# A hybrid attention encoder on one core: fuller contractions, split sums of squares, and other orders at the start, the openings and the end

## The chip, the core and the metric

The kernel runs on one core of a Trainium2 chip. The metric is the device time of the program in microseconds, median of several runs. The core's engines are TensorE (PE; its weight loads are shown apart as PEld), VectorE (DVE), ScalarE (ACT), GpSimd (POOL) and SyncE (SP), which here only issues transfers.

## The reference, cut to what matters

Two layers work on 528 tokens (512 and 16 learned meta tokens) of 1024 channels, in float32:

```python
h = concatenate([meta, x], axis=1)
for l in range(DEPTH):                    # DEPTH = 2
    h = h + 0.5 * swiglu(rmsnorm(h, ...), gate, up, down)     # D_FF = 2816
    h = h + mixer(rmsnorm(h, ...), ...)
    h = h + 0.5 * swiglu(rmsnorm(h, ...), gate, up, down)
return rmsnorm(h, final_norm)[:, N_META:]

def mixer(z, ...):
    h = z @ w_in      # q,k,v,r of branch A, two low-rank decays (16 each), q,k,v of branch B, two gates
    a = gla_branch(...)        # 4 heads, chunked linear attention forwards and backwards
    b = attention_branch(...)  # 8 query heads on 2 key heads, softmax over all 528 tokens
    y = sigmoid(g_a + b0) * (a @ w_pa) + sigmoid(g_b + b1) * (b @ w_pb)
    return y @ w_out
```

In branch A the decay is log_sigmoid(lr @ w2 + b2) / 16 for either direction, and each head's output is normalised by its mean square over 128 channels. In branch B queries and keys are normalised over 64 channels.

## The kernel before, in words

Activations lie with channels on the 128 partitions and tokens along the free axis: eight chunks h(c) of 528 columns, two halves of 264. In the last layer's end only 512 tokens are kept (halves of 256).

**Precision.** A float32 product is made of three matmuls of a reduced type: each operand is split in hi (a cast on ScalarE) and lo (value minus hi, a subtraction on VectorE), and hi·hi, hi·lo and lo·hi are added in PSUM. Some small products are left in full float32: the sums of squares over channels (`means`, L388, and L1016 at the end), the decay product (L612), and the products inside branch A (L655, L691, L718, L727, L728).

**Weights.** The class `Weights` streams slabs of 128x1024 in the order of a plan. Slabs are fetched up to six and made (split) up to four ahead of their use, with four buffers each for hi and lo: the hi cast is L222, the lo subtraction L227. With the flag `by_dma` (the gate projections behind the attention) lo is made by a negation on ScalarE (L224) and an adding transfer issued by POOL (L178).

**Feed-forward.** Gate and up projections work on pairs of 128-wide column blocks with seven products of block sums in place of eight (products "1" to "7", 24 matmuls each, L502). The sums of weights come by chained adding transfers on POOL's queue (`sums`: s3 = block 21 minus block 11, s2 = block 22 plus s3, and so on; products 7, 6, 5, 3 read them), those of activations from `Norm.pair`, which prepares seven operands for each pair of chunks. Products are evaluated in an order that starts "1 2 6 5" for a group's first pair. Products 1, 6, 7 and 4 add up in one PSUM tile (snapshots by ScalarE between them, L508), 2 in a second, 5 and 3 in a third. The down projection follows in groups of 4, 4 and 3 pairs (L382); its results are scaled (L469), added to h (L478), squared (L416) and the squares added up (L420) for the next norm; `Norm.pair` casts (L433) and subtracts (L434) the next operands. `norm.rs()` makes the factors from `means`; it is asked for at high priority behind product 5 of the first pair.

**Mixer.** Projections go through `project` (L382). `gla_pair` is called for two pairs of heads: for each direction a decay product (L612), exponentials and scans (L622), decayed keys (L651) and their transposes (L655), states, then blocks from the last to the first. `attention` normalises and rotates queries and keys, and for each of 16 units of two query blocks makes probabilities (`probs`, L836 and L837) and weighted values (`weighted`): transposes (L861), split, matmuls over four blocks of 128 tokens (L878, L879), and a tail over the 16 meta tokens.

**Order.** Instructions are put in order for each engine ahead of time, by a list scheduler with priorities from the program's order and modelled durations. On the chip each engine then works strictly in that order and waits where data is late. Gate projections are taken in between the attention's units where TensorE has room.

**End.** The last down product (m = 7) is done by halves, and the final norm's factors, multiplications (L1023) and stores (L1025) follow for each half.

## Time and profile before

| | |
|---|---|
| median of three runs | 2294.09 us (2293.67 to 2300.5) |
| span of the profiled execution | 2289.1 us; its own time is not shown apart, the median is 5.0 longer |
| TensorE busy | 2225.1 us, 16548 matmuls |
| VectorE busy | 1491.3 us |
| ScalarE busy | 1214.4 us |
| POOL busy | 195.1 us |
| mean granted clock of TensorE | 0.991 |
| HBM | 264.38 MB read, 2.10 MB written |

A row of a group or of the timeline reads: start and length in us (timeline), engine, line, operation, tile written <- tiles read, shape, count. A TensorE row's length is the latency of overlapping matmuls; the distance of starts is the pitch. In brackets stands the idle time ahead of the instruction and what ended it. Lines are those of the kernel printed above.

### The profile page before, as it was taken

Reading aid. Unit: us, or ns where it says so; the run is one execution under the profiler, and the core shown is the slowest. Engines: PE = TensorE matmul, PEld = TensorE weight load, DVE = VectorE, ACT = ScalarE, POOL = GpSimd, SP = SyncE. Lnnn points to the kernel's source line nnn. Section 1 sums busy time; section 2 is a strip of 40 time slices with the busy share of each in tenths; the row PEclk is TensorE's granted clock in tenths of the full one; section 3 lists DMA queues with packets and bytes.
Section 4 is the critical chain, followed back from the end, with each engine's and each line's share of the span. In section 5 each row is a group of like instructions: output and inputs, shape, how many; then the busy total and the mean of one; then the engine's idle time right before and its main releaser. Section 6 shows DMA issues by size and latency. Waiting matters only on the chain.

```text
span 2289.1 us, 39919 instructions
## 1 busy us (share of the span) xinstructions
PE 2225.1 (97%) x16548; PEld 2108.4 (92%) x16548; DVE 1491.3 (65%) x2355; ACT 1214.4 (53%) x1785; POOL 195.1 (9%) x218
## 2 busy tenths in 40 slices
PE   5999999999999999999989999999999999999997
PEld 5999999989999999999989999998788888989896
DVE  6656567476775676565676565674768667756566
ACT  7536355344786564453565353553448946636452
POOL 1111010010000010101011110100000001101010
PEclk9999999999999999999989999999999999999999
DMA  8858562211325485766667585632113356859661
GB/s 225 236 150 224 142 175 93 74 57 56 84 56 157 117 214 153 189 180 173 181 141 202 151 219 146 170 98 74 56 65 93 74 156 152 223 149 223 159 176 61
DMA packets 91869, 327.79 MB, mean 143 GB/s; under 512 B 10214, under 2 KB 12646, under 8 KB 91688
## 3 DMA queue, kind: packets, MB, share of 16 engines
q1 hardware_dynamic: 61136, 218.26, 28.7%
q0 software_dynamic: 28800, 104.87, 25.6%
q8 instruction: 130, 2.13, 0.4%
q10 hardware_dynamic: 1752, 2.11, 0.3%
q14 instruction: 51, 0.42, 0.1%
HBM read 264.38 MB, written 2.10 MB: 116 GB/s over the span
## 4 chain that ended last, share of the span: by engine, by line
PE 89%; DVE 5%; DMA 2%; ACT 2%; issue 1%; SPq 0%; DVEq 0%; POOL 0%; ACTq 0%
PE ss L502 36%; PE ss L382 27%; PE mm L382 14%; PE sm L382 3%; PE sm L861 1%; PE sm L878 1%; DVE wlo L227 1%; PE sm L879 1%; PE ss L836 1%; DMA w<-win 1%; PE ss L837 1%; PE ss L388 1%; DMA s<-win 1%; PE ss L718 1%; DMA w<-s 1%
## 5 line engine op out<-in xcount | busy, mean ns | idle before, releaser
L502 PE MATMUL ss<-xc,whi 128*128 128x264 f32 (+1 forms) x4928 | 902.3, 285 | 26.5 <-ACT snap L508 9.7
L502 PEld LDWEIGHTS ss<-xc,whi 128*128 128x128 f32 x4928 | 766.8, 189 | 29.3 <-ACT snap L508 10.3
L502 PE MATMUL ss<-xc,wlo 128*128 128x264 f32 (+1 forms) x2464 | 702.1, 285 | 4.3 <-DVE wlo L227 4.3
L382 PE MATMUL ss<-g,whi 128*128 128x264 f32 (+2 forms) x2668 | 494.2, 301 | 0.0
L502 PEld LDWEIGHTS ss<-xc,wlo 128*128 128x128 f32 x2464 | 466.0, 189 | 5.3 <-DVE wlo L227 5.1
L382 PEld LDWEIGHTS ss<-g,whi 128*128 128x128 f32 x2668 | 388.6, 188 | 17.4
L382 PE MATMUL mm<-x,whi 128*128 128x264 f32 (+1 forms) x1712 | 383.5, 315 | 0.0
L222 ACT CAST whi<-w 128x1024 fp32r<-128x1024 f32 (+1 forms) x221 | 230.8, 1047 | 263.1 <-PE ss L382 118.7
L222 ACT CAST whi<-raw 128x1024 fp32r<-128x1024 f32 x190 | 199.3, 1049 | 299.5 <-PE mm L382 106.9
L227 DVE TENSOR_TENSOR wlo<-w,whi 128x1024 fp32r<-128x1024 f32 (+1 forms) x221 | 267.9, 1218 | 110.7 <-ACT whi L222 108.4
L382 PE MATMUL ss<-g,wlo 128*128 128x264 f32 (+2 forms) x1334 | 309.9, 301 | 0.0
L382 PEld LDWEIGHTS mm<-x,whi 128*128 128x128 f32 x1712 | 279.5, 189 | 18.8 <-issue 2.1
L382 PE MATMUL mm<-x,wlo 128*128 128x264 f32 (+1 forms) x856 | 267.2, 317 | 0.0
L227 DVE TENSOR_TENSOR wlo<-raw,whi 128x1024 fp32r<-128x1024 f32 x166 | 203.1, 1224 | 95.2 <-ACT whi L222 94.2
L382 PEld LDWEIGHTS ss<-g,wlo 128*128 128x128 f32 x1334 | 213.4, 188 | 8.7
L227 DVE TENSOR_TENSOR wlo<-s,whi 128x1024 fp32r<-128x1024 f32 x88 | 107.6, 1223 | 102.0 <-ACT whi L222 101.9
L222 ACT CAST whi<-s 128x1024 fp32r<-128x1024 f32 x88 | 92.4, 1050 | 153.6 <-PE ss L502 135.4
L382 PEld LDWEIGHTS mm<-x,wlo 128*128 128x128 f32 x856 | 160.4, 189 | 10.8 <-issue 2.2
L469 DVE SCALAR_TENSOR_TENSOR t<-ss,rs 128x528 f32<-128x528 f32 (+1 forms) x95 | 66.0, 700 | 127.8 <-PE ss L382 127.7
L173 ACT ACTIVATE s<-w 128x1024 f32<-128x1024 f32 x88 | 93.3, 1060 | 79.2 <-DMA w<-win 41.5
L178 POOL DMA_DIRECT2D s<-win x44 | 40.8, 927 | 497.0 <-ACT s L173 489.2
L508 ACT COPY snap<-ss 128x528 f32<-128x528 f32 (+1 forms) x132 | 77.2, 585 | 0.0
(235 smaller groups left out, 2660.3 us busy)
## 6 DMA issues: line engine op xcount, KB each, us to landing
w<-win SPq DMA_DIRECT2D x219, 512.0 KB, 4.7
raw<-wts SPq DMA_DIRECT2D x190, 512.0 KB, 3.4
s<-win POOLq DMA_DIRECT2D x44, 512.0 KB, 6.8
w<-s POOLq DMA_DIRECT2D x44, 512.0 KB, 5.5
w<-win POOLq DMA_DIRECT2D x44, 512.0 KB, 7.1
s<-w POOLq DMA_DIRECT2D x44, 512.0 KB, 7.4
wlo<-raw POOLq DMA_DIRECT2D x24, 512.0 KB, 4.4
h<-xt SPq DMA_DIRECT2D x3, 528.0 KB, 7.1
```

Of the source, the lines that this page charges most:

```text
L173: self.nc.scalar.activation(t, w, AF.Copy, scale=-1.0)
L178: self.nc.gpsimd.dma_start(t, src, accum_op=ALU.add)
L222: nc.scalar.copy(hi[:, cs], w[:, cs])
L227: nc.vector.tensor_tensor(lo[:, cs], w[:, cs], hi[:, cs].bitcast(F32), ALU.subtract)
L382: TE.matmul(acc.half[i][:width], lhs, rhs[:, acc.spans[i]], start=first, stop=last)
L388: TE.matmul(a, weights, x[:, hs], start=True, stop=True)
L469: V.scalar_tensor_tensor(cut(dst[rows]), pv[rows], -0.5 * f, cut(rs[rows]), ALU.mult, ALU.mult)
L502: TE.matmul(acc[:, j], a[:, j, k], b[:, at], start=bool(begin and k == 0 and i == 0), stop=k == len(x) - 1 and i == 2, skip_group_check=no ...
L508: S.copy(st[name], acc)
L718: TE.matmul(ats[:n, hh, d * n : (d + 1) * n], prods[d][1][rows, bs], prods[d][0][rows, bs], start=True, stop=True)
L836: TE.matmul(s[:n, i, :HF], lhs, kh[:, hs], start=True, stop=False)
L837: TE.matmul(s[:n, i, :HF], lhs, kl[:, hs], start=False, stop=True)
```

## The change

- `weighted`: the tail's two matmuls over 16 rows become one over 128: hi of the probabilities in rows 0 to 15, lo in rows 32 to 47, zeros elsewhere; the values stand in both places. Two halves of one buffer are used in turn.
- Decay product: weights and operand are laid out over 128 rows (hi and lo of each, the bias), in the reduced type, one matmul for each half. The low-rank projection computes hi and lo columns side by side (64 columns, two matmuls a chunk and half and no third).
- States: matmuls take all 128 rows, with zeros where a direction has no state. The four score products of a block alternate between heads.
- Sums of squares: `means` becomes `totals`: the squares are split in hi and lo, two matmuls of the reduced type each against ones; the division goes into the later steps.
- `by_dma` goes: all lo slabs are made by VectorE.
- First feed-forward: the first pair is computed from whole blocks (`Norm.whole`, `first_pair`: 192 matmuls, no sums of weights or activations); the seven operands are made behind that.
- The three other feed-forwards open with products 1 and 2 of pair 0 (the last chunk's matmuls of both at the end), then 1 and 2 of pair 1, then 6, 5, 7, 4, 3 of pair 0. For the last chunk the operands are made ahead of the square. The norm's factors are asked for behind product 6.
- End: the last three down products (m = 5, 6, 7) are done by halves, all three for the first half and then for the second; their squares are summed by TensorE in full float32, finished chunks are scaled by ScalarE, and a half is multiplied and stored in two pieces.

```diff
+        if g:
+            steps += [("P", pair, c) for c in "1265"]
+        elif begin:
+            steps += [("F", pair, "1"), ("F", pair, "2")] + [("P", pair + 1, c) for c in "1265"]
+        else:
+            steps += [("O", pair, "12")] + [("P", pair + 1, c) for c in "12"] + [("P", pair, c) for c in "65"]
...
-                if self.by_dma:
-                    nc.scalar.activation(lo[:, cs], hi[:, cs].bitcast(F32), AF.Copy, scale=-1.0)
-                    self.add(lo[:, cs].bitcast(F32), w[:, cs])
-                else:
-                    nc.vector.tensor_tensor(lo[:, cs], w[:, cs], hi[:, cs].bitcast(F32), ALU.subtract)
+                nc.vector.tensor_tensor(lo[:, cs], w[:, cs], hi[:, cs].bitcast(F32), ALU.subtract)
...
+    def totals(weights, x, kind="ss"):
+        n = x.shape[-1]
+        hi, lo = slot("t", F32R, n), slot("t", F32R, n)
+        S.copy(hi, x)
+        V.tensor_tensor(lo, x, hi.bitcast(F32), ALU.subtract)
+        acc = Acc(kind, n)
+        for b, first in ((hi, True), (lo, False)):
+            for a, hs in zip(acc.half, acc.spans):
+                TE.matmul(a, weights, b[:, hs], start=first, stop=not first)
...
         def chunk_of_pair(self, c):
-            self.square(c)
+            if c % 2 and c < KC - 1:
+                self.square(c)
             if c % 2:
                 self.pair(c // 2)
+            if c == KC - 1 or c % 2 == 0:
+                self.square(c)
...
+        def first_pair(p, m):
+            accs = [pair(m == "2") for _ in range(2)]
+            blocks = [W.op((l, f), p, m + c) for c in "12"]
+            for k, (first, second) in enumerate(zip(x, norm.second)):
+                for j, acc in enumerate(accs):
+                    for r, (hi, lo) in enumerate(blocks):
+                        for i, (a, b) in enumerate(((hi, 0), (hi, 1), (lo, 0))):
+                            for t, v in enumerate((first, second)):
+                                TE.matmul(acc[:, t, :w], a[:, j, k], v[b][:, r], ...)
+        def two_products(p, names):
...
+            for ks in (range(last), [last]):
+                for acc, at, hi, lo in work:
+                    for k in ks:
...
-                TE.matmul(z[:, i, :HF], w2t[:33, c0 : c0 + P], lr[:33, hs], start=True, stop=True)
+                TE.matmul(z[:, i, :HF], w2t[:, c0 : c0 + P], lr[:, hs], start=True, stop=True)
...
-                TE.matmul(os_, state(b)[rows, hh], qin[hh][rows, bs], start=False, stop=True)
+                TE.matmul(os_, state(b)[:, hh], qin[hh][:, bs], start=False, stop=True)
...
-                parts.append((vs[g][1], hi[:, :w], lo[:, :w]))
+                S.copy(tail[:META], tp[:META, :w])
+                V.tensor_tensor(tail[32 : 32 + META], tp[:META, :w], tail[:META].bitcast(F32), ALU.subtract)
...
+                TE.matmul(o[:, :w], vs[g][1], tail, start=False, stop=True)
...
-        W.by_dma = True
         gates += [project(x, None, "g", n=n_out) for _ in range(2 * KC - EARLY)]
-        W.by_dma = False
...
+        for i, hs in enumerate(spans):                 # closing: halves
+            for m, acc, wm in zip(late, accs, w):      # m = 5, 6, 7
...
+                    act(sq, h(m, hs), AF.Square)
+                    S.activation(h(m, hs), h(m, hs), AF.Identity, scale=gfin[:, m : m + 1])
...
+        store(0, spans[0])
+        total(1, KC - 1)
+        finish(1)
+        store(1, spans[1])
```

More of the change, by code (lines that the diff above doesn't have):

```diff
@@ L230, in make @@
             self.made += 1
-            if not isinstance(load, int) and load[2] in "12":
+            if not isinstance(load, int) and load[2] in ("1", "2"):
                 self.sums(*load, w)
@@ L503, in product_of_pair, with finished @@
                                   stop=k == len(x) - 1 and i == 2, skip_group_check=not begin)
+            finished(p, product)
+        def finished(p, product):
+            st = made[p]
+            acc = st[{"2": "Y", "5": "Z", "3": "Z"}.get(product, "X")][:, :, :w]
             def snapshot(name):
@@ L547, in down @@
             kind = "s2" if other == (m // 2 % 2 == 1) else "ss"
-            ending = g == len(GROUPS) - 1 and m == KC - 1 and done is None
+            if done is None and g == len(GROUPS) - 1 and m >= LATE:
+                if m == LATE:
+                    closing([hid[base + k] for k in range(2 * GROUPS[g])], rs)
+                return
             if first == 0:
-                sums[m] = Acc(kind, cut=ending)
+                sums[m] = Acc(kind)
             width = 2 * GROUPS[g]
-            product("ffn_w_down", sums[m], [hid[base + k] for k in range(first, last)], last - first, by_half=ending,
+            product("ffn_w_down", sums[m], [hid[base + k] for k in range(first, last)], last - first,
                     begin=first == 0, end=last == width)
-            if last < width or ending:
+            if last < width:
                 return
@@ L983, in build @@
     nc.sync.dma_start(h(1), xt[:, 1])
-    first.pair(0)
-    W.fetch(1)
+    first.whole(0)
+    W.make(2)
     for c in (2, 4, 6):
         nc.sync.dma_start(hall[:, c : c + 2], xt[:, c : c + 2])
-        first.pair(c // 2)
-    W.fetch(2)
-    nc.sync.dma_start(ct[:, C_O1024 : C_O1024 + P], const[:, C_O1024 : C_O1024 + P])
+        first.whole(c // 2)
+    W.make(4)
     for c in range(KC):
         first.square(c)
+    for j in range(KC // 2):
+        first.pair(j)
     norms = [first] + [Norm(G_NORM + i * KC) for i in range(1, 3 * DEPTH)]
```

285 lines of the change are left out of this document (200 added, 85 removed).

## The prediction

> **What bounds the kernel now.** I read the page's head, its engine table and its chain of work first, then the waits of TensorE, then the chain in order of time, and last the timeline around each place that the diff touches.
>
> ```profile
> span 2289.1 us, 39919 instructions
> PE 2225.1 (97%) x16548; PEld 2108.4 (92%) x16548; DVE 1491.3 (65%) x2355; ACT 1214.4 (53%) x1785; POOL 195.1 (9%) x218
> PE 89%; DVE 5%; DMA 2%; ACT 2%; issue 1%; SPq 0%; DVEq 0%; POOL 0%; ACTq 0%
> ```
>
> ```profile
> PE ss L655 <- DVE p L651: 11.8, 8, 2.0
> PE ss L502 <- ACT snap L508: 9.7, 1, 9.7
> PE ss L502 <- ACT whi L222: 9.2, 2, 7.8
> PE ss L502 <- ACT xc L433: 7.3, 1, 7.3
> PE ss L388 <- DVE t L420: 5.4, 3, 2.7
> ...
> PE ss L1016 <- DVE t L1013: 4.3, 2, 2.3
> ```
>
> ```profile
> 160.01 73.19 PE ss L502 x600
> ```
>
> TensorE is busy 97% of the span and is 89% of the chain: the kernel is bound by the number and pitch of its matmuls. The waits (us in total, times, longest) are only some 50 us; the largest lie at the start. The chain row gives the pitch of a full 264-column matmul in a dense stretch: 73.19 / 600 = 0.122 us. So two things can move the time: TensorE work taken away, and the stalls at start, stage openings and end.
>
> **Short contractions (the attention's tail).** Now each block of weighted values ends with two matmuls over 16 rows:
>
> ```profile
> 651.29 0.28 PE L879 MATMUL sm<-q,k 128*128 128x256 f32 x1
> 651.50 0.38 PE L878 MATMUL sm<-lr,vm 16*128 16x256 f32 x1
> 651.73 0.27 PE L879 MATMUL sm<-lr,vm 16*128 16x256 f32 x1
> 651.93 0.51 PE L382 MATMUL mm<-x,whi 128*128 128x264 f32 x2
> 652.28 0.28 PE L836 MATMUL ss<-k,p 128*128 128x264 f32 x1
> ```
>
> From 651.29 to 652.28 are 0.99 us for three full matmuls (0.36) and the two short ones: 0.63 for the pair, because the matmul before the short ones, each of them, and the first behind them all start their successor about 0.1 late. The new form is one full matmul, 0.12. Saved 0.51 here; where transposes follow, rather less, so I take 0.45 for each of 32 calls (two more calls are small): **15 us**, at most 16.3.
>
> The Trainium skill speaks against this: "TensorE: Matmul & The Clock Gate", section "Why this matters for your kernels", says that a single matmul over 32 rows takes the time of one over 128, the gain being only in running several at once. By it one matmul fewer for each of 34 calls would be all, 4 us. No start in the rows above agrees with it; I go by the rows.
>
> **The decay product (L612), sums of squares (L388), states (L728), low rank.**
>
> ```profile
> 481.94 1.05 PE L388 MATMUL ss<-t,const 128*128 128x264 f32 x4
> 482.63 0.48 PE L382 MATMUL mm<-x,wlo 128*128 128x264 f32 x1
> 482.95 0.41 PE L382 MATMUL mm<-x,whi 128*128 128x264 f32 x2
> ...
> 487.39 0.41 PE L382 MATMUL mm<-x,whi 128*128 128x264 f32 x2
> 487.73 1.16 PE L612 MATMUL ss<-lr,w 33*128 33x264 f32 x4
> 488.82 0.39 PE L382 MATMUL mm<-x,wlo 128*128 128x264 f32 x1
> 489.05 0.41 PE L382 MATMUL mm<-x,whi 128*128 128x264 f32 x2
> ...
> 522.17 0.49 PE L728 MATMUL sm<-p,q 64*128 64x128 f32 x2
> 523.00 0.48 PE L728 MATMUL sm<-p,q 64*128 64x128 f32 x2
> ```
>
> ```profile
> L382 PE MATMUL sm<-x,whi 128*32 128x264 f32 x64 | 10.3, 283 | 0.0
> L382 PE MATMUL sm<-x,wlo 128*32 128x264 f32 x32 | 6.4, 282 | 0.0
> ```
>
> L612: 1.66 us from 487.39 to 489.05 less three ordinary pitches is 1.29; the split form is two ordinary matmuls, 0.24. Saved 1.05 x 8 (two pairs, two directions, two layers) = **8.4**. L388: 481.94 to 482.95 is 1.01, less one ordinary pitch 0.89; the hi and lo form is four ordinary ones, 0.49. Saved 0.40 x 16 calls (six norms, eight heads, two key norms) = **6.4**. L728: a short pair and the full pair behind it take 0.83 (522.17 to 523.00); four full matmuls at no more than 0.122 each take 0.49. Saved 0.34 x 8 = **2.7**. Low rank: 96 matmuls become 64, 32 x 0.122 = **3.9**. The swapped order of the score products keeps their number; I give it nothing (0 to 2). Sum of TensorE work taken away: 15 + 8.4 + 6.4 + 2.7 + 3.9 = **36.4 us**.
>
> **What of that comes back as waits.** In the gated branch TensorE already waits 8 times for L651, 11.8 us: the chain of scans and exponentials is what is late there. L612, L728 and half of L388 lie in that branch, 14.3 us; what lies ahead of the chain's first matmul moves the chain too, what lies behind it only lengthens a wait. The nearest row allows anything from 0 to 14.3 lost; I take 3, since most of L612 stands ahead of its chain. The splits add a copy on ScalarE and a subtraction on VectorE to each sum of squares; in the heads other projections cover them, and without that cover they would lengthen the same waits.
>
> The larger risk is the edit that drops by_dma:
>
> ```profile
> 545.00:697.00 152.00, 151.31 (x1168) 141.84 (x1165) 112.22 (x284) 116.70 (x241) 7.42 (x9) 0.99 0.28 74
> 595.00:620.00 25.00, 24.88 (x193) 23.32 (x193) 21.23 (x57) 20.72 (x44) 1.76 (x2) 1.00 0.35 86
> ...
> L224 ACT ACTIVATE wlo<-whi x24: 1040/1062/1092, 584.1 to 1839.6; 128x1024 fp32r<-128x1024 f32 x24
> ...
> L227 DVE TENSOR_TENSOR wlo<-raw,whi 128x1024 fp32r<-128x1024 f32 x166 | 203.1, 1224 | 95.2 <-ACT whi L222 94.2
> ```
>
> 24 slabs get their low half from VectorE (1.224 each) and no longer from ScalarE (1.062) and POOL's queue. The columns after the length are TensorE, weight load, VectorE, ScalarE. In the first attention VectorE has 112.2 of 152 us; nine of the layer's twelve slabs fall there, so 123 of some 144: 85%. In the densest 25 us it has 21.2 now and gets one or two more slabs: 22.4 to 23.7 of the 23.5 that TensorE would then need. So VectorE comes level with TensorE for part of the stage, where TensorE so far waits for nothing. Bounds: 0 (ScalarE's 12.7 us of relief shortens the softmax chain) to all of the attention's gain, 16. I charge 6. Net work: 36.4 - 3 - 6 = **27.4**.
>
> **The start.**
>
> ```profile
> 0.00:40.00 40.00, 16.64 (x81) 14.58 (x82) 29.21 (x54) 31.40 (x53) 4.90 (x10) 0.87 0.84 240
> ...
> 23.00 0.28 PE L502 MATMUL ss<-xc,wlo 128*128 128x264 f32 x1
> 32.99 0.81 PE L502 MATMUL ss<-xc,whi 128*128 128x264 f32 x2 [9.71 <-ACT snap L508]
> 33.60 1.96 PE L388 MATMUL ss<-t,const 128*128 128x264 f32 x4
> ```
>
> In the first 40 us TensorE does 77 matmuls and one sum: 9.4 + 0.9 us of warm work, so 29.7 us are lost. The 9.7 are not snap's: product 6 waits for weights summed by two chained transfers. The first pair from whole blocks needs 192 matmuls for 168 (+24 x 0.122 = 2.9) but no summed weights, so the transfers of pair 1 run under them. It needs two blocks before the first k is complete: start at some 8.5 instead of 7.75. Then 192 x 0.122 = 23.4, about 2.4 more for some 24 of them at half clock (the four records of 33.60 take 1.96, those of 481.94 take 1.05), 1.5 of gaps while chunks arrive: end at 35.8. VectorE's 29.2 and ScalarE's 31.4 busy us in those 40 grow by the second halves' casts and the first pair's low parts, so pair 1's operands come late at its product 6: 3 us charged (0 to 9.7, the wait that stands there now). Lost then 35.8 + 3 - 168 x 0.122 = 18.3; gain 29.7 - 18.3 = **11** (5 to 17).
>
> **Openings with four products.**
>
> ```profile
> 1169.32 0.70 DVE L469 SCALAR_TENSOR_TENSOR t<-ss,rs 128x528 f32<-128x528 f32 x1
> 1170.17 0.78 PE L502 MATMUL ss<-xc,whi 128*128 128x264 f32 x2 [7.34 <-ACT xc L433]
> 1175.60 2.12 PE L388 MATMUL ss<-t,const 128*128 128x264 f32 x4 [2.67 <-DVE t L420]
> ```
>
> Between the layers TensorE stands 7.3 us. The profile names the cast, but the first matmul reads only the oldest operand; the eviction L469 at 1169.32 ends at 1170.02, and it frees the bank that pair 0's first product takes. That eviction is not moved, so these 7.3 us stay. Behind it 36 matmuls instead of 18 stand ahead of the last chunk, and that chunk's operand comes ahead of its square: 18 x 0.122 = 2.2 saved, part of the 2.67 too. In the two other openings the waits are the rest of L388's 5.4, 2.7 for both: I count half. Against it, the sum now needs a cast and a subtraction more, and product 7 is followed at once by 4, which must wait for the snapshot of the same bank; pair 1's product 6 can fill that (without this cover 1 us for each of three openings). 2.2 + 1.4 less 0.6: **3** (-3 to 8).
>
> **The end.**
>
> ```profile
> 2272.21 0.28 PE L382 MATMUL ss<-g,wlo 128*128 128x256 f32 x1
> 2274.43 0.70 PE L1016 MATMUL ss<-t,const 128*128 128x256 f32 x2 [1.95 <-DVE t L1013]
> 2277.45 1.02 PE L1016 MATMUL ss<-t,const 128*128 128x256 f32 x2 [2.31 <-DVE t L1013]
> ```
>
> The second half's sum now stands 3.0 behind the first; with the first half done under the second half's products it takes its place, and no squares are added between: 3.4 sooner. Two multiplications of 1024 columns (1.22 each, as L227) replace eight, about 1 sooner at the end. Against it six single sums over full-precision squares (0.45 each, half of L388's 0.89), five of them ahead of the last product, and two splits' four matmuls: 2.7; and the last transfer is twice as large. **1.5** (-1 to 4). The scaling of finished chunks moves to ScalarE, idle there; without that room 0.6 for a chunk.
>
> Costed at nothing: assembling the low-rank and decay operands, the zero fills and gfin; the projections of the same stage cover them, else some 3 us for a layer.
>
> **Sum.** 27.4 + 11 + 3 + 1.5 = 42.9. The span is 2289.1; the median of the runs shown, 2294.1, is 5.0 longer, which I take as what lies around the span. 2294.1 - 42.9 = **2251 us**. All good ends (36.4 + 17 + 8 + 4) give 2229, all bad ones (36.4 - 14.3 - 16 = 6, then + 5 - 3 - 1) 2287.
>
> **Rivals.** *VectorE takes over the attention.* Place: both attention stages; decided where it passes TensorE over the whole stage. For it: 21.2 of 25 us already. Against: no wait of TensorE for it there today, and its mean stays at 85%. The attention's 16 us go: 2251 + 10 = 2261. *The start gains nothing*: both vector engines saturate (31.4 of 40 on ScalarE) and pair 1's product 6 waits the same 9.7: 2262. *Short contractions cost nothing extra*: then the tails save 4 and not 15, L728 nothing, L612 only the repeated passes (four records at L388's 0.89 / 4 become 0.24 in all, 5.2 and not 8.4): 2251 + 17 = 2268. This is the rule of the Trainium skill's TensorE page quoted above; against it stand the starts of the tail rows. *Slower*: the sums and casts on an in-order VectorE make TensorE wait in every one of the attention's 34 weighted calls. Priced at the longest wait for L651, 2.0 us: 68, so 2251 - 6 (charged already) being replaced by it, 2313. It decides the sign from 1.5 us for each call on. Against it: 85% mean load, and a ScalarE that is relieved.
>
> **Chances.** My forecast 0.52; VectorE 0.20; start 0.12; no switching cost 0.04; slower 0.08; several losses at once, ending within 0.3%, 0.04. A difference of 0.3% (7 us) is about what a measurement can tell from none. The first four are faster: 0.88; slower 0.08. The range takes the first four cases in with their bounds: 2234 to 2272.
>
> **What would show it.** No 16-row or 33-row matmul in the list; a pitch of 0.12 around the tail; no single idle of TensorE over 5 us in the first 40 us; the 7.3 us before product 1 of layer 1 still there; VectorE at 85 to 90% in the attention. Waits of TensorE for VectorE in the attention adding up to over 16 us, or a wait of over 10 us behind the first pair, would make the number wrong.

## The result, and the profile after

The changed kernel takes 2263.92 us (median of four runs, 2259.63 to 2265.68), the kernel before 2295.72 beside it: a ratio of 0.986, 95% interval 0.984 to 0.9875. That is 1.4% faster, on the side forecast and within the range of 2234 to 2272, but 12.9 us above the 2251 predicted.

The head and the engine table of the changed kernel's page, and its waits of TensorE (us in total, times, longest):

```profile
span 2261.6 us, 39885 instructions
PE 2204.5 (97%) x16538; PEld 2102.9 (93%) x16538; DVE 1527.2 (68%) x2397; ACT 1218.3 (54%) x1824; POOL 164.7 (7%) x184
```

```profile
PE ss L764 <- DVE p L760: 12.5, 8, 2.1
PE ss L597 <- ACT whi L238: 9.5, 4, 4.7
PE ss L556 <- ACT whi L238: 8.0, 2, 7.2
PE ss L597 <- ACT snap L608: 7.4, 4, 3.8
PE ss L597 <- DVE wlo L239: 5.1, 6, 2.2
PE ss L1136 <- ACT square L387: 1.4, 1, 1.4
```

The gated branch's wait stands as before (11.8, now 12.5 at L764). The 9.7 at the start and the 7.3 between the layers are gone, and so are the waits for the squares. In their place come waits of products (L597) for weights (whi, wlo) and for snapshots (snap): 22 us, of which 18 lie behind the first group, where no such wait stood before. L597 is the old L502, L404 the old L382.

The span, 27.5 us shorter, cut at the first and last matmul of each stage (worked out from the starts in the timeline; a mixer is counted from its first projection to the start of `w_out`, which is in "all else"):

| stage | before | after | gain | predicted |
|---|---|---|---|---|
| start to the end of the first group | 160.0 | 151.3 | 8.7 | 11 |
| mixer, layer 0 | 375.2 | 366.0 | 9.2 | |
| mixer, layer 1 | 353.7 | 336.5 | 17.2 | 27.4 for both |
| first groups of the three later feed-forwards | 400.2 | 409.5 | -9.3 | +3 |
| last groups and end (from 2179.5 before) | 109.6 | 107.3 | 2.3 | 1.5 |
| all else | 890.4 | 891.0 | -0.6 | 0 |

The openings are the row with the wrong sign: 12.3 of the 15.4 us by which the span (2289.1 - 42.9 = 2246.2 predicted, 2261.6 measured) came out longer. The start adds 2.3, the mixers 1.0 and all else 0.6, and the end takes 0.8 off. That the medians differ by only 12.9 is luck: the 5.0 us taken as lying around the span came from a median and a profile of different executions. Seven later runs of the kernel before have 1.8 to 2.0 us around their spans, the changed kernel's profiled run 1.9 (2263.49 against 2261.6); with 2.0 the forecast would have been 2248.

**The start.** One row of a windows view, to be held against the row for the same 40 us before (TensorE 16.64 us, 81 matmuls), and the first long wait of the changed kernel in the timeline:

```profile
0.00:40.00 40.00, 31.39 (x228) 30.78 (x228) 31.14 (x61) 33.80 (x60) 3.69 (x8) 1.00 0.78 240
```

```profile
7.20 0.59 PE L556 MATMUL ss<-xc,whi 128*128 128x264 f32 x1 [7.20 <-ACT whi L238]
9.64 0.59 PE L556 MATMUL ss<-xc,whi 128*128 128x264 f32 x1 [0.75 <-ACT whi L238]
...
61.86 0.51 PE L597 MATMUL ss<-xc,whi 128*128 128x264 f32 x2 [3.80 <-ACT snap L608]
```

From the first matmul on, the first 40 us are nearly full, as forecast; the first pair ends at 34.8 us. A wait of 3.8 us, about the size of the 3 charged, stands at 58 us. It isn't the one that was charged: the product at 61.86 is the eighth behind the first pair, product 4 of pair 1, and it waits for a snapshot that ScalarE takes late.

**The opening between the layers**, rows of all engines from the changed kernel's timeline:

```profile
1148.40 1.06 ACT L238 CAST whi<-w 128x1024 fp32r<-128x1024 f32 x1 [1.94 <-PE ss L404]
...
1164.28 1.04 ACT L238 CAST whi<-w 128x1024 fp32r<-128x1024 f32 x1
...
1165.35 1.23 DVE L239 TENSOR_TENSOR wlo<-w,whi 128x1024 fp32r<-128x1024 f32 x1 [0.23 <-ACT whi L238]
...
1166.61 5.94 SPq L184 DMA_DIRECT2D w<-win  x4
...
1170.56 0.86 POOL L194 DMA_DIRECT2D w<-s  x1 [32.28 <-DVE c L615]
1173.27 0.89 POOL L194 DMA_DIRECT2D w<-win  x1 [1.85 <-DMA w<-win]
...
1177.05 1.04 ACT L238 CAST whi<-w 128x1024 fp32r<-128x1024 f32 x1 [2.42 <-DMA w<-s]
...
1178.14 0.51 PE L597 MATMUL ss<-xc,whi 128*128 128x264 f32 x2 [2.23 <-ACT whi L238]
...
1182.26 1.04 ACT L238 CAST whi<-w 128x1024 fp32r<-128x1024 f32 x1 [4.16 <-DMA w<-win]
...
1183.35 0.81 PE L597 MATMUL ss<-xc,whi 128*128 128x264 f32 x2 [4.70 <-ACT whi L238]
```

Read from the bottom: the product at 1183.35 waits 4.70 us for a cast of weights, and the cast at 1182.26 waits 4.16 us for the adding transfer that POOL issued at 1173.27. The product at 1178.14 depends in the same way on the transfer of 1170.56, ahead of which POOL issued nothing for 32.28 us.

POOL's row names c (L615), but the transfer doesn't read c: that is only VectorE's last instruction before it. The transfer adds to a block that SyncE has to fetch first. SyncE requests it at 1166.61, right behind VectorE's subtraction of 1165.35 (1165.35 + 1.23 = 1166.58); the waits of SyncE's queue show 18.6 us behind such a subtraction. That subtraction splits the summed weights of pair 0's product 6, and so frees one of the two buffers for short sums.

It comes that late because the slab is the fifth of the opening. Products 1 and 2 of pair 0 and 1 and 2 of pair 1 hold all four buffers of hi and lo from the cast of 1148.40 on. None of the four ends before the last chunk's matmuls, at about 1162 to 1164, and the next slab's cast starts at 1164.28.

**The tail of the attention**, now one full matmul, goes through at the ordinary pitch (0.12 to it and 0.12 from it, where the pair of 16-row matmuls took 0.63):

```profile
643.27 0.28 PE L993 MATMUL sm<-q,k 128*128 128x256 f32 x1
643.39 0.28 PE L994 MATMUL sm<-lr,vm 128*128 128x256 f32 x1
643.51 0.27 PE L976 MATMUL sm<-const,t 128*128 128x128 f32 x1
```

### The profile page after: what moved, and what is told of

It is laid out like the page before. It is cut to its first block, busy times and chain, and to the rows that moved or that the text cites. A ratio compares the mean times of both kernels' runs of the same rounds, so it can differ in the third digit from the quotient of the medians.

```text
span 2261.6 us, 39885 instructions
## 1 busy us (share of the span) xinstructions
PE 2204.5 (97%) x16538; PEld 2102.9 (93%) x16538; DVE 1527.2 (68%) x2397; ACT 1218.3 (54%) x1824; POOL 164.7 (7%) x184
## 5 line engine op out<-in xcount | busy, mean ns | idle before, releaser
L597 PE MATMUL ss<-xc,whi 128*128 128x264 f32 (+1 forms) x4720 | 865.1, 285 | 16.9 <-ACT whi L238 9.5
L597 PEld LDWEIGHTS ss<-xc,whi 128*128 128x128 f32 x4720 | 734.7, 189 | 19.7 <-ACT whi L238 10.3
L597 PE MATMUL ss<-xc,wlo 128*128 128x264 f32 (+1 forms) x2360 | 671.4, 285 | 5.1 <-DVE wlo L239 5.1
L404 PE MATMUL ss<-g,whi 128*128 128x264 f32 (+1 forms) x2620 | 482.8, 300 | 0.0
L597 PEld LDWEIGHTS ss<-xc,wlo 128*128 128x128 f32 x2360 | 446.8, 189 | 6.4 <-DVE wlo L239 6.3
L404 PEld LDWEIGHTS ss<-g,whi 128*128 128x128 f32 x2620 | 380.6, 188 | 15.7
L404 PE MATMUL mm<-x,whi 128*128 128x264 f32 (+1 forms) x1712 | 385.8, 315 | 0.0
L239 DVE TENSOR_TENSOR wlo<-raw,whi 128x1024 fp32r<-128x1024 f32 x190 | 232.1, 1222 | 105.8 <-ACT whi L238 104.8
L404 PE MATMUL ss<-g,wlo 128*128 128x264 f32 (+1 forms) x1310 | 302.2, 300 | 0.0
L404 PEld LDWEIGHTS mm<-x,whi 128*128 128x128 f32 x1712 | 281.2, 190 | 15.3 <-DVE x L393 0.2
L404 PE MATMUL mm<-x,wlo 128*128 128x264 f32 (+1 forms) x856 | 265.2, 314 | 0.0
L404 PEld LDWEIGHTS ss<-g,wlo 128*128 128x128 f32 x1310 | 209.2, 188 | 8.3
L404 PEld LDWEIGHTS mm<-x,wlo 128*128 128x128 f32 x856 | 161.2, 190 | 7.6
L527 DVE SCALAR_TENSOR_TENSOR t<-ss,rs 128x528 f32<-128x528 f32 (+1 forms) x93 | 64.6, 700 | 126.4 <-PE ss L404 126.3
L194 POOL DMA_DIRECT2D w<-win x43 | 37.8, 880 | 599.3 <-DVE wlo L239 222.3
L393 DVE TENSOR_TENSOR g<-c,g 128x528 fp32r<-128x528 f32 (+1 forms) x88 | 61.5, 699 | 22.6 <-ACT g L392 22.6
```

What stands on the lines that cost most here:

```text
L194: self.nc.gpsimd.dma_start(t, src, accum_op=ALU.add)
L239: nc.vector.tensor_tensor(lo[:, cs], w[:, cs], hi[:, cs].bitcast(F32), ALU.subtract)
L393: V.tensor_tensor(lo, src, hi.bitcast(F32), ALU.subtract)
L404: TE.matmul(acc.half[i][:width], lhs, rhs[:, acc.spans[i]], start=first, stop=last)
L527: V.scalar_tensor_tensor(cut(dst[rows]), pv[rows], -0.5 * f, cut(rs[rows]), ALU.mult, ALU.mult)
L597: TE.matmul(acc[:, j], a[:, j, k], b[:, at], start=bool(begin and k == 0 and i == 0), stop=k == len(x) - 1 and i == 2, skip_group_check=no ...
```

## The experiments

All stand against the changed kernel (2263.92 us, span 2261.6) and are edits of it. The kernel before took 2292.9 to 2293.7 us beside them and 2295.7 beside the changed kernel, so medians that differ by less than some 3 us tell nothing. Where stage lengths are compared they are cut as in the table above. "Opening sum" is the first groups of the three later feed-forwards together: 400.2 before, 409.5 after.

### The scaling of the ones moved out of the start

```diff
     def load_constants():
-        S.activation(ones64, b64, AF.Copy, scale=float(HD))
...
+        if l == 0:                       # in the attention
+            S.activation(ones64, b64, AF.Copy, scale=float(HD))
```

> The changed kernel with one instruction moved: the scaling of the 64-channel ones, which load_constants puts on ScalarE right behind the request for the constants, is made ahead of the first attention. Theory A (ScalarE stands 4.7 us for the constants' transfer at 54 to 59 us, the snapshot behind it is late, TensorE waits 3.8 us and then runs 3.4 us at half clock): the wait of 3.8 us behind the first pair goes and the time falls by 4 to 6 us. Theory B (TensorE waits there for the weights summed by chained transfers, the constants only happen to land then): a wait of about the same size stays at product 6 or 5 of pair 1, and the time moves by less than 2 us.

2262.43 us, span 2258.8. The wait of 3.80 us at product 4 of pair 1 is gone: the scaling, queued on ScalarE behind the constants' load, did hold the snapshot. But two products later, at product 6 of pair 2, 2.05 us behind a cast of summed weights stand at 62.8 us, and the first group takes 143.7 us (144.1). The transfers held the start nearly as long as the scaling did, and the time is as long as before, as the second theory had it.

### The openings with two products again

```diff
-        if g:
+        if g or not begin:
             steps += [("P", pair, c) for c in "1265"]
...
-        else:
-            steps += [("O", pair, "12")] + [("P", pair + 1, c) for c in "12"] + [("P", pair, c) for c in "65"]
```

> The changed kernel with the three later feed-forwards opened as before (products 1, 2, 6, 5 of pair 0); all else stays, the operands ahead of the last square and the split sums too. Theory A (four products ahead move product 6 of pair 0 nearer to product 6 of pair 1, and with two buffers for short sums the chained transfers of pair 1 come late): the first groups of these feed-forwards, which take 134.1, 145.5 and 129.9 us from the end of the product before, go back to 131, 141 and 126, and the time falls by 8 to 12 us. Theory B (the later square and the longer chain of the split sum hold TensorE up): the groups stay within 2 us of 134.1, 145.5 and 129.9.

Span 2249.9, opening sum 398.3 (131.0 + 141.3 + 126.0). The waits of this kernel:

```profile
PE ss L593 <- ACT xc L484: 7.3, 1, 7.3
PE ss L411 <- ACT t L406: 4.4, 3, 1.8
PE ss L593 <- ACT snap L604: 1.8, 2, 1.5
```

The waits for weights in the openings have gone and the old 7.3 us between the layers are back: the four products cost 11.2 us of opening, more than the 7.3 and the waits for squares that they remove. The median, 2260.93 (2252.08 to 2261.45), fell by only 3, not by the 8 to 12 expected: the profiled run is the fastest of the four, the others were granted a clock of 0.988 to 0.989 and not 0.992.

### The low halves by ScalarE and POOL again in the gates

```diff
+                if self.by_dma:
+                    nc.scalar.activation(lo[:, cs], hi[:, cs].bitcast(F32), AF.Copy, scale=-1.0)
+                    self.add(lo[:, cs].bitcast(F32), w[:, cs])
+                else:
                     nc.vector.tensor_tensor(lo[:, cs], w[:, cs], hi[:, cs].bitcast(F32), ALU.subtract)
```

> The changed kernel with the low halves of the late gate slabs made again by ScalarE and an adding transfer, as before. Theory A of the prediction (VectorE comes level with TensorE in the attention and costs some 6 us of its gain): 3 to 6 us faster. Theory B (VectorE has room, ScalarE was the fuller engine): within 2 us, or slower by up to 4 us since ScalarE gets 12.7 us more in each layer.

2266.41 us, span 2268.4: not faster, so the first theory fails. Attention to the last weighted values takes 232.9 us for both layers against 235.0, the projections behind it 119.9 against 116.8. The 2.1 us are no cost of VectorE: the attentions of the changed kernel hold 708 matmuls of projections, those of this kernel 687, and 21 matmuls are 2.6 us at 0.122. Together the two parts take 352.8 us here and 351.8 in the changed kernel. The densest 26 us of the changed kernel in the windows view (TensorE, weight load, VectorE, ScalarE), and of this one:

```profile
584.00:610.00 26.00, 25.88 (x210) 25.09 (x210) 25.41 (x62) 18.48 (x40) 0.00 (x0) 1.00 0.19 62
```

```profile
584.00:610.00 26.00, 25.64 (x200) 24.71 (x199) 23.11 (x61) 21.48 (x44) 1.75 (x2) 0.96 0.34 87
```

VectorE is busy 98% there after the change, and TensorE is busy 25.88 of the 26 us all the same. Here a full VectorE costs TensorE nothing that the rows show.

### Two 16-row matmuls in the tail again

```diff
...
+                parts.append((vs[g][1], hi[:, :w], lo[:, :w]))     # 16 rows each
...
-                TE.matmul(o[:, :w], vs[g][1], tail, start=False, stop=True)
```

> The changed kernel with the attention's tail as before: two matmuls over 16 rows for each of 34 calls, in one buffer. Theory A (a short contraction costs by the switch into it and out of it): 16-row matmuls with starts 0.2 us apart are back, 0.35 to 0.45 us for each of 32 calls, 11 to 15 us slower. Theory B (a short contraction costs what a full one does, only their number counts): 34 matmuls more at 0.12, 4 us slower.

2276.29 us (2267.5 to 2287.45), 12.4 slower than with one full matmul. That the 12.4 lie in the forecast's 11 to 15 says little: the runs spread by 20 us, with granted clocks from 0.984 to 0.994, and the profiled run has 26 us more at half clock than the changed kernel's, none of it in the attention. The stage itself, measured with the next experiment, is 8.4 us longer, between the two theories. The tail in the timeline:

```profile
640.82 0.28 PE L989 MATMUL sm<-q,k 128*128 128x256 f32 x1
641.03 0.38 PE L988 MATMUL sm<-lr,vm 16*128 16x256 f32 x1
641.25 0.28 PE L989 MATMUL sm<-lr,vm 16*128 16x256 f32 x1
641.45 0.33 PE L971 MATMUL sm<-const,t 128*128 128x128 f32 x1
```

640.82 to 641.45 is 0.63 for three matmuls, where three full ones take 0.36. The first short one starts 0.21 behind a full one, the second 0.22 behind the first, and the full one 0.20 behind that: each of the three starts is 0.1 late.

### The full tail issued twice

```diff
-                TE.matmul(o[:, :w], vs[g][1], tail, start=False, stop=True)
+                for i in range(2):
+                    TE.matmul(o[:, :w], vs[g][1], tail, start=False, stop=i == 1)
```

> Each tail's one full matmul over 128 rows is issued twice (its terms are then added twice). Theory A (a 16-row matmul costs by the switch between row counts, not by being one matmul more): the second full matmul costs one pitch, 34 x 0.12 = 4 us, so 4 above the after kernel's span at the same clock and 8 to 10 below the kernel with two 16-row matmuls. Theory B (a matmul over few rows takes the time of one over 128, and the cost lay in having two dependent on late operands): as long as the kernel with 16-row matmuls, the two attention stages (first probabilities to last weighted values, 123.9 and 111.1 us with one full matmul) both 6 or more longer; by A they are 2 longer each.

2269.16 us, span 2270.9, with 17 us more at half clock than the changed kernel's profile has, so the stage is compared here too, not the span. The tail in the timeline:

```profile
648.68 0.28 PE L993 MATMUL sm<-q,k 128*128 128x256 f32 x1
648.79 0.40 PE L995 MATMUL sm<-lr,vm 128*128 128x256 f32 x2
649.03 0.29 PE L951 MATMUL ss<-k,p 128*128 128x264 f32 x1
```

Two full matmuls take 0.24 (648.79 to 649.03), where the two short ones take 0.42 and delay their entry by 0.1. From the first probabilities to the last projection, both layers: 351.8 us with one full matmul, 355.5 with two, 360.2 with two of 16 rows. One full matmul more costs 3.7 (34 x 0.122 is 4.1), making the two short costs another 4.7. So it isn't the number: in this attention two 16-row matmuls between full ones cost more than two of 128 rows. By the pitches of the tail and of the score products ahead of it the difference of the last two is 8.5; the stages show 4.7. With the short ones, the other matmuls of the stage take 2.8 us less by their pitches and TensorE idles 0.9 less; why they do, no run shows.

### Pair 1's products 1 and 2 back between pair 0's steps

```diff
-            steps += [("O", pair, "12")] + [("P", pair + 1, c) for c in "12"] + [("P", pair, c) for c in "65"]
+            steps += [("O", pair, "12")] + [("P", pair, c) for c in "65"]     # 1 and 2 of pair 1 by 7 and 4, as before
```

> The three later blocks still open with products 1 and 2 of pair 0 interleaved, but pair 1's 1 and 2 move back to where pair 0's steps 7 and 4 stand, so that seven products instead of five lie between product 6 of pair 0 and product 6 of pair 1. Theory A (the openings lose by the distance: pair 1's summed weights come too late): the waits behind the opening go, the first groups of those three blocks fall from 134.1 + 145.5 + 129.9 = 409.5 us to some 398 (they were 398.3 without the four products), the span from 2261.6 to about 2250. Theory B (they lose by the interleaving itself, for instance by both banks being taken at once, wherever pair 1's products stand): they stay at 407 to 410, the span within 3 us of 2261.6.

2254.1 us, span 2252.8, opening sum 400.5 (131.8 + 142.7 + 126.0). Interleaving the two products of pair 0 is thus not what costs, as the first theory had it. With seven products between the sixes (counted from the start of pair 0's product 6 to the start of pair 1's) the openings are as long as before the change, and the 7.3 us between the layers are back.

### Three products ahead

```diff
-            steps += [("O", pair, "12")] + [("P", pair + 1, c) for c in "12"] + [("P", pair, c) for c in "65"]
+            steps += [("O", pair, "12")] + [("P", pair + 1, "1")] + [("P", pair, c) for c in "65"]     # 2 of pair 1 by 4
```

> Three products ahead of pair 0's 6 and 5: 1 and 2 of pair 0 interleaved, then 1 of pair 1; its 2 moves back to the place between 7 and 4. Six products lie between the two 6s. Theory A (distance): between the two others, first groups 399 to 404 us in all, span 2251 to 2256; the third product ahead of the layer boundary's eviction may fill part of the 7.3 us that stand there without pair 1's products, then 392 to 397. Theory B (the interleaving): 407 to 410 as with four.

2246.93 us (2244.44 to 2250.95), ratio to the kernel before 0.980 (0.9787 to 0.9817); span 2245.0, opening sum 392.5 (130.0 + 137.5 + 125.0), better than before the change and than either neighbour. Between the layers the timeline's idle of TensorE is:

```profile
1149.02 1.10 PE L597 MATMUL ss<-xc,whi 128*128 128x264 f32 x2 [3.62 <-ACT xc L488]
1151.27 0.78 PE L580 MATMUL ss<-xc,whi 128*128 128x264 f32 x2 [0.27 <-DVE t L527]
...
1159.73 0.51 PE L415 MATMUL ss<-t,whole 128*128 128x264 f32 x2 [0.91 <-ACT t L410]
```

The third product (L597, of pair 1, by the code in another PSUM tile) goes first, and only then L580 waits 0.27 for the eviction (L527, the old L469); that halves the 7.3. The weights' chains come in time here. Pair 0's product 6 is the fourth slab and not the fifth: its cast starts at 1143.73, with the opening, where the changed kernel's starts 15.8 us into it.

### Four products, but one more before pair 1's product 6

```diff
+            if g == 0 and i == 1 and not begin:
+                early = [[], early[1]]
...
             if more:
-                steps += [("P", p + 1, "6"), ("P", p + 1, "5")]
+                ahead = not begin and g == 0 and i == 0
+                steps += [("P", p + 2, "1")] * ahead + [("P", p + 1, "6"), ("P", p + 1, "5")]
```

> The opening keeps its four products as in the after kernel; only pair 2's product 1 moves from behind pair 1's 6 and 5 to ahead of them, so that six products instead of five lie between product 6 of pair 0 and that of pair 1 (2.9 us more, 24 matmuls at 0.122). Theory A (distance): the waits of 0.9 to 4.7 us some 23 to 35 us into the openings shrink by up to 2.9 each, the three first groups come to 398 to 403 us in all (409.5 with five, 392.5 with three products and a distance of six), the span to 2251 to 2256. Theory B (what costs is that two products of pair 1 stand ahead of pair 0's 6 and 5, whatever the distance): 407 to 411, the span within 3 of 2261.6.

2256.61 us, span 2250.3, opening sum 400.8 (131.8 + 139.8 + 129.2). One product of distance gives back 8.7 of the 17.0 us that lie between four and three products. The waits in the opening between the layers have shrunk from 2.23 and 4.70 to about 1 each:

```profile
1173.55 1.01 PE L600 MATMUL ss<-xc,whi 128*128 128x264 f32 x4 [1.01 <-ACT whi L241]
1181.70 0.51 PE L600 MATMUL ss<-xc,whi 128*128 128x264 f32 x2 [0.92 <-DVE c L644]
```

The other 8.3 us lie in what two products of pair 1 (not one) ahead of pair 0's 6 and 5 do. The traces show what that is, though no run changes it alone. In us from the opening's start, between the layers and, in brackets, in the two other openings:

| products ahead | cast of the weights of pair 0's product 6 | first sum for pair 1 landed |
|---|---|---|
| two | -4.3 (-1.4, -1.4) | 8.0 (9.9, 10.4) |
| three | 0.0 (0.0, 0.0) | 12.5 (12.5, 14.2) |
| four | 15.8 (7.1, 6.8) | 28.5 (21.8, 21.9) |
| four, one product more distance | 15.8 (7.1, 6.8) | 26.9 (21.1, 21.9) |

With two or three products ahead the slab of product 6 is among the first four, for which there are buffers; with four it waits until one of the products ahead has ended, and the sums for pair 1 with it. The distance then decides how much of that delay TensorE sees.

The two outer openings together, which have no 7.3 us to win, take 256.9 to 257.9 us in the three kernels with two products, 255.0 and 255.1 in the two with three, 263.1 to 265.5 in all seven with four products and a distance of five, and 261.0 here. There the fourth product costs some 9 us, and one product of distance gives back about 3.

### The squares ahead of the operands again

```diff
         def chunk_of_pair(self, c):
-            if c % 2 and c < KC - 1:
-                self.square(c)
+            self.square(c)
             if c % 2:
                 self.pair(c // 2)
-            if c == KC - 1 or c % 2 == 0:
-                self.square(c)
```

> At the openings each chunk's square is taken ahead of its operand again, as before the change; the four products stay. Theory A (the order of square and operand is worth what I gave it, part of the last chunk's wait): the first groups of the three later blocks get 1 to 2 us longer each, span +3 to +6. Theory B (with four products ahead of it, the last chunk's operand is never what is late): no difference over 1 us in the three first groups together.

Both expectations missed: 2255.72 us, span 2253.3, opening sum 401.9 (133.0 + 137.0 + 131.9), 7.6 shorter. All of it lies between the layers (145.5 to 137.0): the idle there falls from 11.8 to 4.4, and the half-clock stretch from 10.2 to 3.4. The other two openings have single waits of 2.75 and 4.14 for snapshots. What moved is the timing of POOL's adding transfers, issued 0.4 to 1.7 us earlier from the stage's start. With a chain that is just late, a reordering that has nothing to do with it moves several microseconds; the order itself I can't price from this. It also means that the 5.7 us between the layers (145.5 to 139.8) of the run above can't be put down to the distance alone: here 8.5 us went with the distance unchanged. The two other openings, 264.9 us together against 264.0, didn't gain.

### The start as before the change, with two-product openings

```diff
-            steps += [("F", pair, "1"), ("F", pair, "2")] + [("P", pair + 1, c) for c in "1265"]
...
-    first.whole(0)
-    W.make(2)
+    first.pair(0)
+    W.fetch(1)
...
-    for j in range(KC // 2):
-        first.pair(j)
```

> The first block opens as the three others did before the change (first pair by the seven summed products, operands in the old order) and the three later blocks open as before too; to be read against the kernel without the four-product openings (span 2249.9; first group 141.4 us from the first matmul, openings 131.0, 141.3, 126.0). Theory A (whole blocks gain by doing without the summed weights at the start): the first group goes back to about 152 us, the wait of 9 to 10 us for summed weights is back at the first pair's product 6, span about 2260. Theory B (the gain of the first group comes from the other edits at the start: one transfer for the constants, split sums): the first group stays at 142 to 147, span within 5 of 2249.9.

Span 2262.1, first group 151.4 us against 141.4 of the other kernel with two-product openings. The wait for summed weights is back at the first pair's product 6, 7.19 us long and not 9 to 10:

```profile
19.09 0.39 PE L593 MATMUL ss<-xc,wlo 128*128 128x264 f32 x1 [0.81 <-DVE wlo L235]
29.97 0.81 PE L593 MATMUL ss<-xc,whi 128*128 128x264 f32 x2 [7.19 <-ACT snap L604]
```

The row names the snapshot, but ScalarE only reaches it at 29.33 us, behind two casts of weights that began at 27.43, when the transfer into w had landed. The start from whole blocks is worth 10.0 us, as the first theory had it.

### The sums of squares in full precision

```diff
     def totals(weights, x, kind="ss"):
-        hi, lo = slot("t", F32R, n), slot("t", F32R, n)
-        S.copy(hi, x)
-        V.tensor_tensor(lo, x, hi.bitcast(F32), ALU.subtract)
-        for b, first in ((hi, True), (lo, False)): ...
+        TE.matmul(a, weights.bitcast(F32), x[:, hs], start=True, stop=True)     # for each half
```

> The sums of squares of the norms and heads are again one full-precision matmul for each half, without the cast and the subtraction; all else as in the after kernel. Theory A (each of the 16 calls is worth the 0.40 us of the prediction, nothing waits for the cast): span 2261.6 + 6.4 = 2268. Theory B (worth what the pitches of the after kernel show, 14.0 us for all calls before and 9.6 after): 4.4 longer in matmuls, and up to 3 us shorter waits behind the splits, so 2263 to 2266. Theory C (the splits cost more in waits than the matmuls save): below 2259, with the waits in the gated branch, 12.5 us, shrinking by 2 or more.

2266.57 us, span 2269.1. A call in this kernel and half a call (two of its four matmuls) in the changed one:

```profile
470.98 1.08 PE L411 MATMUL ss<-t,whole 128*128 128x264 f32 x4
471.70 0.48 PE L404 MATMUL mm<-x,whi 128*128 128x264 f32 x1
```

```profile
474.66 0.40 PE L415 MATMUL ss<-t,whole 128*128 128x264 f32 x2
474.90 0.41 PE L404 MATMUL mm<-x,whi 128*128 128x264 f32 x2
```

A call takes 0.72 in full precision. Split, the half shown takes 0.24 and the other half of the same call 0.35, 0.59 together. Over the 16 calls the pitches are 11.8 and 9.6 us (14.0 before the change, where two calls ran at half clock). The two mixers are 4.8 and 4.9 us longer; 5.0 of that are more stretches at half clock, some 4.7 remain. The second theory comes nearest: the 6.4 of the prediction are too many, and no wait pays for the split.

### Three products and the ones moved

```diff
-            steps += [("O", pair, "12")] + [("P", pair + 1, c) for c in "12"] + [("P", pair, c) for c in "65"]
+            steps += [("O", pair, "12")] + [("P", pair + 1, "1")] + [("P", pair, c) for c in "65"]
...
-        S.activation(ones64, b64, AF.Copy, scale=float(HD))        # moved to the attention
```

> Three products at the openings and the scaling of the ones moved out of the start. Theory A (the start is held by the chained sums for pair 2, not by the scaling): span 2242 to 2246, no faster than three products alone (2245.0) by more than 3 us, first group 143 to 145. Theory B (with both, the start's wait goes): first group 140 to 142, span 2240 to 2242.

2246.29 us, span 2244.7, the same as three products alone, as the first theory had it; for the first group the second was right. The start's wait is nearly gone and the first group 141.4 us long, 2.9 shorter:

```profile
63.83 0.51 PE L596 MATMUL ss<-xc,whi 128*128 128x264 f32 x2 [0.45 <-ACT whi L238]
65.09 0.39 PE L596 MATMUL ss<-xc,wlo 128*128 128x264 f32 x1 [0.75 <-DVE wlo L239]
```

The gain was lost in mixer 0, where the stage of the decays took 66.6 us and not 64.5, with more time at half clock (450.6 to 457.4 and 491.5 to 494.9, against 455.4 to 458.8 alone).

## Why the prediction came out as it did

**What bounds the kernel: right.** TensorE stays at 97%, and the gains lie where its work or its idle went.

**Openings: the step that failed** (+3 forecast, -9.3). I counted what stands ahead of the last chunk and let pair 1's product 6 "fill" the bank wait behind 7; I did not ask when that product's weights come, and priced their delay at nothing. They are sums by chained adding transfers, into buffers that pair 0's summed weights leave. With four products ahead all four buffers of split slabs are taken, pair 0's product 6 is split 7 to 16 us later than with three, and the sums for pair 1 with it. At the same time two products of pair 1 taken forward leave five between the sixes where seven stood, 5.9 us less (2 x 24 x 0.122), so TensorE arrives sooner. The 9.3 are 5.8 more idle (12.7 to 18.5 over the three openings), 1.7 more for work at half clock, and 1.8 over. The 1.8 are about what ten more waits cost beyond the idle shown, by my estimate: a record of 0.28 is 0.16 longer than a pitch.

That the fourth product costs is shown by the runs with two and three (opening sums 398.3, 400.5 and 392.5), and the interleaving is cleared by the run that keeps it with two. The distance is shown to matter by some 3 us in the outer openings; that the buffers make the rest is read from the traces and not tested by a run of its own. I was also wrong about the 7.3 us between the layers, in the other direction: I said that they stay, but pair 1's products (L597) don't need the bank that the late eviction frees, and they run first (a wait of 2.24 is left with four products, 3.62 with three).

**Mixers: the sum right (27.4, measured 26.4), two terms wrong.** By the pitches of each shape, both layers:

| term | predicted | measured |
|---|---|---|
| tails (with the score products ahead) | 15 | 12.5 |
| decay product | 8.4 | 5.9 |
| sums of squares, all 16 | 6.4 | 4.4 |
| states | 2.7 | 3.6 |
| low rank | 3.9 | 3.9 |
| sum | 36.4 | 30.3 |

I priced each short group from a single place, up to the second or third matmul behind it, and subtracted ordinary pitches. That put delays of that place on the group: the tail saves 0.39 a call (0.63 less 0.24 in the rows of the experiment), not 0.45; L612 took 1.09 a call, not 1.29, and its replacement takes 0.35, not 0.24. Against this, the charges for what comes back (3 in the gated branch, 6 for VectorE) were not needed: that branch's wait went from 11.8 to 12.5, and TensorE waits 0.3 us in each attention. So one error of 6 hid another of some 8. The balance doesn't close: 30.3 less 2.7 for the sums outside the mixers, 2.1 more idle of all kinds and 1.8 for more half clock (6.8 us of it before, 10.3 after) is 23.7, and 2.7 of the measured 26.4 I can't assign.

**Short contractions: the row was right, the rule not enough.** The rule of the Trainium skill that I weighed ("TensorE: Matmul & The Clock Gate", "Why this matters for your kernels") made the tails worth 4. The stage is 8.4 us longer with the 16-row form (12.4 by medians, which half clock elsewhere inflates), and 3.7 longer with one full matmul more. The Trainium skill's page "TensorEngine Tiling (Array Packing)", section "Key Properties", says that changing the tiling mode drains the engine. It gives no figure, and no run here shows whether a 16-row matmul is such a change. It could be behind the 0.1 us on entry and the 0.1 on exit, but not behind the third, between the two short ones.

**Start: right in kind.** 10.0 us by the run that undoes it, 8.7 in the changed kernel's profile, 11 predicted; what is missing goes with the wait at 58 us and a half-clock stretch behind it. That the 3 charged for a wait is near the 3.8 measured is luck. I charged it at pair 1's product 6 for operands made late by a full VectorE and ScalarE; product 6 waits 0.3 there. The wait came at pair 1's product 4, for a snapshot behind the constants' load, and with that out of the way at pair 2's product 6, for summed weights.

**End:** 1.5 forecast, 2.3 measured. **Rivals:** VectorE did not take over (98% in its densest 26 us, 82% over the first attention, 102.26 of 124 us, and no wait); the start did gain; the slower case had no sign of its per-call wait.

## What to carry to other kernels

When products are moved forward, count what lies between two uses of a late resource and not only what lies ahead of the stall that you attack: here a fourth product ahead took the last buffer of split weights, the first sum for the next pair landed 8 to 16 us later, and with a distance of five products to their use that cost 9 us in place of a gain. When a row names what ended a long wait, check that the instruction needs it: POOL's row named an addition, and what held it was a fetch by SyncE. Price a short group over all its calls and not from one row's surroundings. A stage's idle may be filled from the other buffer's work (three products: 3.6 left of 7.3) without borrowing the whole distance.

## What was not expected of the hardware

The clock. In the changed kernel's windows view (PEclk is the third number from the end):

```profile
59.30:62.70 3.40, 0.84 (x7) 0.84 (x8) 2.67 (x4) 2.50 (x5) 0.00 (x0) 1.00 0.93 247
62.70:66.10 3.40, 3.40 (x18) 3.40 (x17) 1.81 (x3) 2.40 (x3) 0.88 (x1) 0.50 0.12 27
66.10:69.50 3.40, 3.40 (x30) 3.40 (x29) 3.40 (x6) 2.53 (x6) 0.88 (x1) 1.00 1.02 164
...
810.20:813.60 3.40, 1.76 (x12) 1.33 (x12) 1.23 (x1) 1.04 (x1) 1.75 (x2) 1.00 0.95 205
...
574.70:578.10 3.40, 3.40 (x31) 3.27 (x29) 2.01 (x7) 2.14 (x6) 0.00 (x0) 1.00 0.00 0
578.10:581.50 3.40, 3.40 (x18) 3.25 (x17) 2.10 (x7) 1.40 (x4) 0.00 (x0) 0.50 0.00 0
```

At a clock of 0.50 each stretch of 3.4 us costs up to 1.7 us, and the clock's records show stretches of 3.4, 6.8, 10.2 and 13.7 us, with starts a multiple of 3.41 us apart within a run. The Trainium skill ("TensorE: Matmul & The Clock Gate", "What's actually happening") describes a free-running window of about 3.4 us, which agrees; it lets the throttle return after an idle window, but here windows with 0.84 or 1.76 us of work were enough (59.30 and 810.20, the second with no single wait above some 0.9 us), and between 574.70 and 578.10 TensorE was busy throughout by the profile. So a wait of 2 us costs, by where it falls, nothing, 1.7 or more on top: profiled runs of kernels that differ by one edit differ by up to 6.8 us in places that the edit doesn't touch. That is why a stage was judged by its idle and its pitches, and not by the span alone.
